# Activations stored as two halves, even and odd tokens, and read by the matmuls from both halves in turn

## The chip, the cores and the metric

The kernel runs on one core of one Trainium2 chip. The metric is the device time of one execution in microseconds (us), lower is better. The profile names the engines PE (TensorE matmuls), PEld (TensorE weight loads, which overlap PE), DVE (VectorE), ACT (ScalarE), POOL (GpSimd) and SP (SyncE, which issues most of the DMAs).

## The reference, cut to what matters

One decoder layer is computed for 288 tokens: a prompt of 256 tokens and 8 samples of 4 tokens. The width is 2048, the feed-forward width 5632.

```python
h = _rms(x, g_mix) * (1 + sc_m) + sh_m
proj = h @ w_in
b_gate, c_gate, hc, u, v, ga, gb = jnp.split(proj, idx, axis=-1)
# short convolution -> ya, spatial gating -> yb
merged = jax.nn.sigmoid(ga) * (ya @ w_pa) + jax.nn.sigmoid(gb) * (yb @ w_pb)
x = x + gt_m * (merged @ w_out)
h2 = _rms(x, g_ffn) * (1 + sc_f) + sh_f
gate, up = jnp.split(h2 @ w_ffn_in, 2, axis=-1)
x = x + gt_f * ((jax.nn.silu(gate) * up) @ w_ffn_out)
```

The shifts, scales and gates come from `silu(c) @ w_ada + b_ada`. Everything is in float32.

## The kernel before, in words

**Layout.** Activations are held transposed: features on the 128 partitions, tokens along the free axis. A tile of activations is therefore 128 x 288 (`T` = 288), and 128 x 298 (`TU`) where nine columns of modulation vectors and one of zeros ride along.

**The split matmul.** To keep float32 accuracy, each operand is split in two numbers of a shorter float type (`F32R`, fp32r in the profile): `hi`, a rounded copy, and `lo`, what is left. A product is three matmuls into one PSUM tile: weight hi by activation hi, weight hi by activation lo, weight lo by activation hi. The weight tile (128 x 128) is the stationary operand, the activation tile the moving one, read column by column.

- `Blk.run` (lines 464 to 478) is the main form. Lines 474, 475 and 476 are the three matmuls, inside a loop over output tiles and over the tiles of the contraction.
- `FirstBlk.run` (481 to 494) does the first block of w_in, with its matmul on line 492: 8 output tiles by three matmuls, all of 298 columns.
- `KBlk.run` (498 to 516) does the first four output tiles of the feed-forward input, in 4 blocks of 4 contraction tiles by 4 output tiles by three matmuls (lines 508 to 510), all of 298 columns.

**Where activation halves are made.** ACT copies to `hi`, DVE subtracts to `lo`. This is done in `split` (222), in `Modulate.high` and `Modulate.low` (271 and 275), in `modulate` (280) and in `early0` (583). `split` is called by `scaled` (249), `mix_conv` (675), `gate` in `spatial` (763), `sink_pb` (787) and `sink_fi` (829). Altogether 1 + 16 tiles of 298 columns are split and 16 + 16 + 8 + 8 + 16 + 44 = 108 tiles of 288. A split activation tile is read by every output tile of its matrix, so its two halves are made once and streamed into TensorE many times.

**Weights** are split likewise, in segments of up to 512 columns (`Blk.high`, 433, and `Blk.low`, 445). The change does not touch these.

**Other matmuls** are the modulation `Ada` (`Ada.run`, line 352, matmul on line 364), which reads unsplit float32 weights as the moving operand, and small sums, transposes and broadcasts. They read their operands as before.

**Order.** The order of the whole work is a hand-written list, `steps`. On DVE, ACT and SP a wrapper `Pinned` (line 103) keeps instructions in the written order until the list ends it; every instruction issued through it carries the line number 114 in the profile. On TensorE, `behind(S["pe"])` keeps blocks in order. Weights come by DMA from the SP queue, five buffers ahead (`RAW`).

Of the kernel before, what the change touches and what calls it, by code (L numbers as in the profile page):

```python
# [7 lines left out]
F32 = mybir.dt.float32  # L8
F32R = mybir.dt.float32r
ALU = mybir.AluOpType  # L10
AF = mybir.ActivationFunctionType

P = 128
D = 2048
T = 288
TP = 256
TU = T + 10
# [62 lines left out]
def _body(tc, nc, d, pc, pw, pslot, ptmp, pps):  # L80
    ids = [0]

    def nm(s):
        ids[0] += 1
        return f"{s}_{ids[0]}"
# [4 lines left out]
    def slot(dt=F32, shape=(P, T)):  # L90
        return pslot.tile(list(shape), dt, tag="s", name=nm("s"), padded_shape=[P, TU])

    def tmp(n=T):
        return ptmp.tile([P, n], F32, tag="t", name=nm("t"), padded_shape=[P, TU])

    def psmain():
        return pps.tile([P, 512], F32, tag="main", name=nm("pm"), bufs=4)

    def psmisc():
        return pps.tile([P, 512], F32, tag="misc", name=nm("px"), bufs=3)  # L100

    def behind(i):
        return tc.issue_after(i.ins) if i is not None else ExitStack()
# [17 lines left out]
    V, A, G, PE, SY = Pinned(nc.vector), Pinned(nc.scalar), nc.gpsimd, nc.tensor, Pinned(nc.sync)  # L121
# [94 lines left out]
    def sam(ap):  # L216
        return ap.rearrange("p (b s) -> p b s", s=NS)

    def bc4(ap):
        return ap.unsqueeze(2).to_broadcast([P, NB, NS])  # L220

    def split(a, n=T):
        hi = slot(F32R, (P, n))
        S["hi"] = A.copy(hi, a)
        lo = slot(F32R, (P, n))
        S["lo"] = V.tensor_tensor(lo, a, hi.bitcast(F32), ALU.subtract)
        return hi, lo

    def normed(kt, rb):
        t = slot()  # L230
# [3 lines left out]
    def in_order(i):  # L234
        if S["strict"]:
            S["pe"] = i
        return i
# [19 lines left out]
    class Modulate:  # L257
# [11 lines left out]
            S["aff"] = G.tensor_tensor(sam(h[:, TP:]), sam(h[:, TP:]), bc4(mod[:, sh, 1:]), ALU.add)  # L269

        def high(self):
            self.hi = slot(F32R)
            A.copy(self.hi, self.h)

        def low(self):
            lo = slot(F32R)
            V.tensor_tensor(lo, self.h, self.hi.bitcast(F32), ALU.subtract)
            self.out[self.k] = (self.hi, lo)

    def modulate(ks, get, gm, sh0, out):  # L280
        hs, his = {}, {}

        def affine(k, t):
            h = tmp()
            A.activation(
                h[:, :TP], t[:, :TP], AF.Identity, bias=mod[:, sh0 + k, 0:1], scale=gm[:, k, 0:1]
            )
            G.tensor_tensor(sam(h[:, TP:]), sam(t[:, TP:]), bc4(gm[:, k, 1:]), ALU.mult)  # L288
            S["aff"] = G.tensor_tensor(sam(h[:, TP:]), sam(h[:, TP:]), bc4(mod[:, sh0 + k, 1:]), ALU.add)  # L289
            hi = slot(F32R)  # L290
            A.copy(hi, h)
            hs[k], his[k] = h, hi

        def finish_(k):
            lo = slot(F32R)
            V.tensor_tensor(lo, hs[k], his[k].bitcast(F32), ALU.subtract)
            out[k] = (his[k], lo)

        ts = {}
        n = len(ks)  # L300
        for i in range(n + 2):
            if i < n:
                ts[i] = get(ks[i])
            if 1 <= i <= n:
                affine(ks[i - 1], ts.pop(i - 1))
            if i >= 2:
                finish_(ks[i - 2])
# [22 lines left out]
    class Ada(Step):  # L330
# [21 lines left out]
        def run(self):  # L352
            w, ks = self.nq * 128, self.ks
            if self.blk == 0:
                Ada.cur[self.name] = pps.tile([P, 512], F32, tag="ada", name=nm("ada"), bufs=1)
            acc = Ada.cur[self.name]
            for k, h in [(k, h) for k in range(self.nk // ks) for h in range(1 + self.apart)]:
                for j in range(4):
                    kt = self.blk * self.nk + k * ks + j % ks
                    o = (k * 4 + j) * w  # L360
                    c = slice(256 * h, 256 * h + 256) if self.apart else slice(0, w)
                    with behind(S.get("pe")):
                        self.last = in_order(
                            PE.matmul(  # L364
                                acc[32 * j : 32 * j + 32, c],
                                cs[:, kt, :],
                                self.raw[2 * j + h] if self.apart else self.raw[:, o : o + w],
                                start=(kt < ks),
                                stop=(kt >= 16 - ks),
                                tile_position=(0, 32 * j),  # L370
                                skip_group_check=True,
                            )
                        )
            if (self.blk + 1) * self.nk == 16 and not self.defer:
                self.tail()
# [31 lines left out]
    class Blk(Step):  # L407
# [56 lines left out]
        def run(self):  # L464
            cuts = self.cuts or [0, self.nk]
            acc = {}
            for a, b, j in [(a, b, j) for a, b in zip(cuts, cuts[1:]) for j in range(self.nm)]:
                ps = acc[j] if a else acc.setdefault(j, psmain())
                for k in range(a, b):
                    wh, wl = self.parts[j * self.nk + k]  # L470
                    ah, al = self.rhs(self.k0 + k)
                    first, last = k == 0, k == self.nk - 1
                    with behind(S.get("pe")):
                        PE.matmul(ps[:, : self.n], wh, ah, start=first, stop=False)  # L474
                    PE.matmul(ps[:, : self.n], wh, al, start=False, stop=False)  # L475
                    self.last = in_order(PE.matmul(ps[:, : self.n], wl, ah, start=False, stop=last))  # L476
                if b == self.nk:
                    self.sinks(j, ps)

    class FirstBlk(Blk):  # L480
        def run(self):
            ah, al = self.rhs(0)
            cuts = [0] + list(range(2, self.nm + 1))
            for a, b in zip(cuts, cuts[1:]):
                pss = [psmain() for _ in range(a, b)]
                for n in range(3):
                    for i, ps in enumerate(pss):
                        wh, wl = self.parts[a + i]
                        w, r = ((wh, ah), (wl, ah), (wh, al))[n]
                        with behind(S.get("pe")):  # L490
                            self.last = in_order(
                                PE.matmul(ps[:, : self.n], w, r, start=n == 0, stop=n == 2)
                            )
                for i, ps in enumerate(pss):
                    self.sinks(a + i, ps)

    class KBlk(Blk):
        def run(self):
            if self.idx == 0:
                S["kps"] = [psmain() if j else psmisc() for j in range(self.nm)]  # L500
            nb = 16 // self.nk
            for k in range(self.nk):
                ah, al = self.rhs(self.idx * self.nk + k)
                first, last = self.idx + k == 0, self.idx == nb - 1 and k == self.nk - 1
                for j in range(self.nm):
                    ps = S["kps"][j]
                    wh, wl = self.parts[k * self.nm + j]
                    PE.matmul(ps[:, :TU], wh, ah, start=first, stop=False)
                    PE.matmul(ps[:, :TU], wh, al, start=False, stop=False)
                    self.last = PE.matmul(ps[:, :TU], wl, ah, start=False, stop=last)  # L510
                for f in self.then.get(k, ()):
                    f()
            if self.idx == nb - 1:
                for j, ps in enumerate(S.pop("kps")):
                    self.sink(j, ps)
# [20 lines left out]
    S = {"strict": True}  # L536
# [46 lines left out]
    def early0():  # L583
        a = S["x0"] = tmp(TU)
        G.memset(a[:, T + NC :], 0.0)
        gain1(0, 1)
        V.tensor_scalar(a[:, :TP], x[:, 0, :TP], gm1[:, 0, 0:1], None, ALU.mult)
        V.tensor_tensor(sam(a[:, TP:T]), sam(x[:, 0, TP:]), bc4(gm1[:, 0, 1:]), ALU.mult)
        G.tensor_copy(a[:, T : T + NC], mod[:, 0, :])
        G.tensor_tensor(  # L590
            a[:, T + 1 : T + NC], a[:, T + 1 : T + NC], a[:, T : T + 1].to_broadcast([P, NB]), ALU.subtract
        )
        wA[0].high()
        hi = slot(F32R, (P, TU))
        A.copy(hi, a)
        wA[0].low()
        lo = slot(F32R, (P, TU))
        V.tensor_tensor(lo, a, hi.bitcast(F32), ALU.subtract)
        xe[0] = (hi, lo)
        wA[0].high()  # L600
        wA[0].low()

# [15 lines left out]
    xe, sq = {}, {}  # L618
# [387 lines left out]
    n = len(steps)  # L1006
# [163 lines left out]
```

## Time and profile before

| what | value |
|---|---|
| median of 3 runs | 1632.2 us (1631.9 to 1632.58) |
| profiled execution: span, the one time that its page gives | 1630.9 us |
| PE busy | 1618.2 us, 99% of the span |
| PEld busy | 1554.6 us, 95% |
| DVE busy | 995.3 us, 61% |
| ACT busy | 740.7 us, 45% |
| POOL busy | 121.2 us, 7% |
| read from HBM | 352.56 MB, 218 GB/s over the span |

The span is the stretch covered by the profiled execution's instructions. The median of the timed runs is 1.3 us longer. Matmuls are pipelined: the duration that the profile gives for one is the time from its start until its last result is written, and the next one starts well before that. So the cost of a matmul in a dense stream is read from the distance between starts, not from its duration. For groups, the columns are: line, engine, operation, out<-in, shapes and count; then busy time in us and mean ns of one; then idle time of the engine just before the group, and what ended it.

### The profile page before, as it was taken

Reading aid. Unit: us, or ns where it says so; the run is one execution under the profiler, and the core shown is the slowest. Engines: PE = TensorE matmul, PEld = TensorE weight load, DVE = VectorE, ACT = ScalarE, POOL = GpSimd, SP = SyncE. Lnnn points to the kernel's source line nnn. Section 1 sums busy time; section 2 is a strip of 40 time slices with the busy share of each in tenths; the row PEclk is TensorE's granted clock in tenths of the full one; section 3 lists DMA queues with packets and bytes.
Section 4 is the critical chain, followed back from the end, with each engine's and each line's share of the span. In section 5 each row is a group of like instructions: output and inputs, shape, how many; then the busy total and the mean of one; then the engine's idle time right before and its main releaser. Section 6 shows DMA issues by size and latency. Waiting matters only on the chain.

```text
span 1630.9 us, 31703 instructions
## 1 busy us (share of the span) xinstructions
PE 1618.2 (99%) x12584; PEld 1554.6 (95%) x12584; DVE 995.3 (61%) x2003; ACT 740.7 (45%) x1373; POOL 121.2 (7%) x251
## 2 busy tenths in 40 slices
PE   9999999999999999999999999999999999999997
PEld 7898899998999998999989899999999999999997
DVE  5776577877655566657845455555555555555565
ACT  5443354643444444446734344444444444344453
POOL 2267010000100000012200000000000000000000
PEclk9999999999999999999999999999999999999999
DMA  9877765766877777764588545443464434545342
GB/s 359 337 263 295 301 260 179 260 240 261 306 286 275 255 258 273 242 233 168 196 280 294 203 169 204 167 162 135 163 211 158 170 135 161 208 159 178 124 169 76
DMA packets 74468, 357.70 MB, mean 219 GB/s; under 512 B 8416, under 2 KB 28288, under 8 KB 44112
## 3 DMA queue, kind: packets, MB, share of 16 engines
q1 hardware_dynamic: 73968, 354.95, 60.6%
q8 instruction: 98, 1.61, 0.4%
q0 software_dynamic: 352, 0.73, 0.1%
q14 instruction: 50, 0.41, 0.1%
HBM read 352.56 MB, written 3.09 MB: 218 GB/s over the span
## 4 chain that ended last, share of the span: by engine, by line
issue 51%; ACT 0%; DVE 0%; POOL 0%; POOLq 0%; PE 0%; DVEq 0%
DVE x L114 0%; ACT hi L114 0%; ACT t L114 0%; ACT s L114 0%; POOL t L288 0%; POOL t L289 0%; PE px L211 0%; POOLq L1156 0%; DVE lo L114 0%; DVE s L114 0%; DVEq L1156 0%; DVEq L114 0%; POOLq L288 0%
## 5 line engine op out<-in xcount | busy, mean ns | idle before, releaser
L474 PE MATMUL pm<-s,hi 128*128 128x288 f32 (+1 forms) x3704 | 1094.4, 295 | 0.3 <-ACT s L114 0.2
L476 PE MATMUL pm<-s,lo 128*128 128x288 f32 (+1 forms) x3704 | 1090.3, 294 | 0.0
L475 PE MATMUL pm<-s,hi 128*128 128x288 f32 (+1 forms) x3704 | 1089.6, 294 | 0.0
L114 DVE TENSOR_TENSOR lo<-raw,hi 128x512 fp32r<-128x512 f32 (+1 forms) x966 | 662.2, 687 | 480.2 <-ACT hi L114 465.2
L114 ACT CAST hi<-raw 128x512 fp32r<-128x512 f32 (+1 forms) x966 | 587.0, 608 | 772.7 <-PE pm L475 735.7
L474 PEld LDWEIGHTS pm<-s,hi 128*128 128x128 f32 x3704 | 696.2, 188 | 11.8 <-issue 9.0
L475 PEld LDWEIGHTS pm<-s,hi 128*128 128x128 f32 x3704 | 696.5, 188 | 0.0
L476 PEld LDWEIGHTS pm<-s,lo 128*128 128x128 f32 x3704 | 696.0, 188 | 0.3 <-DVE lo L114 0.3
L364 PE MATMUL ada<-raw,cs 128*32 128x512 f32 (+3 forms) x768 | 75.6, 525 | 1.2 <-DMA raw<-in_aA 0.7
L114 DVE TENSOR_TENSOR s<-pm,s 128x288 f32<-128x288 f32 x128 | 58.1, 455 | 30.0 <-PE pm L476 29.5
L205 POOL TENSOR_TENSOR r<-r,mhalf 128x3 f32<-128x3 f32 x3 | 3.0, 996 | 883.8 <-DVE r L114 883.8
L114 ACT CAST s<-t 128x288 fp32r<-128x288 f32 (+1 forms) x109 | 46.9, 432 | 23.6 <-DVE t L114 19.5
L364 PEld LDWEIGHTS ada<-raw,cs 128*32 128x32 f32 x768 | 21.9, 110 | 36.8 <-issue 30.0
L114 DVE TENSOR_TENSOR s<-t,s 128x288 fp32r<-128x288 f32 (+1 forms) x109 | 50.0, 461 | 8.3 <-ACT s L114 8.3
L114 DVE SCALAR_TENSOR_TENSOR t<-t,pm 128x288 f32<-128x288 f32 x84 | 37.8, 451 | 15.9 <-PE pm L476 15.9
L114 DVE SCALAR_TENSOR_TENSOR x<-pm,mod,x 128x256 f32<-128x256 f32 x80 | 38.0, 475 | 0.0
L613 POOL TENSOR_TENSOR s<-s,rb 128x288 f32<-128x288 f32 x40 | 37.2, 932 | 0.0
L114 DVE TENSOR_TENSOR t<-pm,mod 128x32 f32<-128x32 f32 x80 | 15.3, 192 | 21.0 <-PE pm L476 21.0
L252 POOL TENSOR_TENSOR t<-x,gm 128x32 f32<-128x32 f32 x16 | 7.8, 490 | 268.9 <-DVE acc L114 255.7
L114 DVE SCALAR_TENSOR_TENSOR s<-pm,s 128x288 f32<-128x288 f32 x48 | 24.4, 511 | 0.5
L288 POOL TENSOR_TENSOR t<-s,gm 128x32 f32<-128x32 f32 x28 | 12.2, 437 | 154.1 <-DVE s L114 77.2
L114 ACT ACTIVATE t<-x 128x288 f32<-128x288 f32 x30 | 13.4, 445 | 20.1 <-DVE x L114 20.1
(126 smaller groups left out, 547.6 us busy)
## 6 DMA issues: line engine op xcount, KB each, us to landing
raw<-in_fi SPq DMA_DIRECT2D x84, 1024.0 KB, 4.9
raw<-in_a SPq DMA_DIRECT2D x48, 1024.0 KB, 4.9
raw<-in_f SPq DMA_DIRECT2D x64, 704.0 KB, 4.0
raw<-in_wD SPq DMA_DIRECT2D x36, 1024.0 KB, 8.5
raw<-in_wC SPq DMA_DIRECT2D x20, 896.0 KB, 6.7
raw<-in_aE SPq DMA_DIRECT2D x16, 1024.0 KB, 7.3
s<-in_a SPq DMA_DIRECT2D x128, 128.0 KB, 5.3
raw<-in_wo SPq DMA_DIRECT2D x16, 1024.0 KB, 5.7
```

What stands on the lines that cost most here:

```text
L114: i = f(*args, **kw)
L205: G.tensor_tensor(r, r, mhalf, ALU.pow)
L252: G.tensor_tensor(sam(a[:, TP:T]), sam(x[:, k, TP:]), bc4(gm[:, k, 1:]), ALU.mult)
L288: G.tensor_tensor(sam(h[:, TP:]), sam(t[:, TP:]), bc4(gm[:, k, 1:]), ALU.mult)
L364: PE.matmul(acc[32 * j : 32 * j + 32, c], cs[:, kt, :], self.raw[2 * j + h] if self.apart else self.raw[:, o : o + w], start=(kt < ks), st ...
L474: PE.matmul(ps[:, : self.n], wh, ah, start=first, stop=False)
L475: PE.matmul(ps[:, : self.n], wh, al, start=False, stop=False)
L476: self.last = in_order(PE.matmul(ps[:, : self.n], wl, ah, start=False, stop=last))
L613: G.tensor_tensor(a[:, :T], a[:, :T], S[rb], ALU.mult)
```

## The change: what it does

Two views are defined. `pair` looks at a tile of n columns as n/2 pairs of neighbours; walked in its order it is the natural order of the columns. `turn` looks at a tile as two halves of n/2 columns and walks them in turn: column 0 of the first half, column 0 of the second, column 1 of the first, and so on.

Every `hi` and `lo` tile of activations is now written through `turn` while the source is read through `pair`. So the first half of the tile holds the even tokens, the second half the odd ones. Every split matmul reads its moving operand through `turn`, so its columns come in natural order, and the PSUM tile and all that follows it stay as they were. In the moving operand, neighbouring columns lie n/2 elements apart: 144 x 4 = 576 bytes, or 149 x 4 = 596 bytes for 298 columns. `lo` is subtracted with source, `hi` and result walked in this way.

No instruction is added, removed or moved in the written order; only access patterns change. The weights, the `Ada` matmuls and the small matmuls keep theirs.

```diff
+    def turn(t, n=T):
+        return t[:, :n].rearrange("p (a b) -> p b a", a=2)
+
+    def pair(t, n=T):
+        return t[:, :n].rearrange("p (b a) -> p b a", a=2)
+
+    def upper(a, n=T):
+        hi = slot(F32R, (P, n))
+        A.copy(turn(hi, n), pair(a, n))
+        return hi
+
+    def lower(a, hi, n=T):
+        lo = slot(F32R, (P, n))
+        V.tensor_tensor(turn(lo, n), pair(a, n), turn(hi.bitcast(F32), n), ALU.subtract)
+        return lo
+
     def split(a, n=T):
-        hi = slot(F32R, (P, n))
-        S["hi"] = A.copy(hi, a)
-        lo = slot(F32R, (P, n))
-        S["lo"] = V.tensor_tensor(lo, a, hi.bitcast(F32), ALU.subtract)
-        return hi, lo
+        hi = upper(a, n)
+        return hi, lower(a, hi, n)
...
         def high(self):
-            self.hi = slot(F32R)
-            A.copy(self.hi, self.h)
+            self.hi = upper(self.h)
 
         def low(self):
-            lo = slot(F32R)
-            V.tensor_tensor(lo, self.h, self.hi.bitcast(F32), ALU.subtract)
-            self.out[self.k] = (self.hi, lo)
+            self.out[self.k] = (self.hi, lower(self.h, self.hi))
...
-                    ah, al = self.rhs(self.k0 + k)
+                    ah, al = (turn(t, self.n) for t in self.rhs(self.k0 + k))
...
-            ah, al = self.rhs(0)
+            ah, al = (turn(t, self.n) for t in self.rhs(0))
...
-                ah, al = self.rhs(self.idx * self.nk + k)
+                ah, al = (turn(t, TU) for t in self.rhs(self.idx * self.nk + k))
```

`modulate` and `early0` are changed in the same way, to call `upper` and `lower`.

More of the change, by code (lines that the diff above doesn't have):

```diff
@@ L289, in affine @@
             S["aff"] = G.tensor_tensor(sam(h[:, TP:]), sam(h[:, TP:]), bc4(mod[:, sh0 + k, 1:]), ALU.add)
-            hi = slot(F32R)
-            A.copy(hi, h)
-            hs[k], his[k] = h, hi
+            hs[k], his[k] = h, upper(h)
         def finish_(k):
-            lo = slot(F32R)
-            V.tensor_tensor(lo, hs[k], his[k].bitcast(F32), ALU.subtract)
-            out[k] = (his[k], lo)
+            out[k] = (his[k], lower(hs[k], his[k]))
         ts = {}
@@ L593, in early0 @@
         wA[0].high()
-        hi = slot(F32R, (P, TU))
-        A.copy(hi, a)
+        hi = upper(a, TU)
         wA[0].low()
-        lo = slot(F32R, (P, TU))
-        V.tensor_tensor(lo, a, hi.bitcast(F32), ALU.subtract)
-        xe[0] = (hi, lo)
+        xe[0] = (hi, lower(a, hi, TU))
         wA[0].high()
```

## The prediction

> **What bounds the kernel now.** I read the page first: the span, the busy shares and the row of the granted clock.
>
> ```profile
> span 1630.9 us, 31703 instructions
> PE 1618.2 (99%) x12584; PEld 1554.6 (95%) x12584; DVE 995.3 (61%) x2003; ACT 740.7 (45%) x1373; POOL 121.2 (7%) x251
> PEclk9999999999999999999999999999999999999999
> ```
>
> PE has 12.7 us of idle time in 1630.9, and its clock is full throughout. A busy PE is not yet PE at its peak, so next I read the table of busy time by stretch, in which the columns after each stretch are PE, PEld, DVE, ACT and POOL with their counts, then clock, DMA share and GB/s.
>
> ```profile
> 100.00:300.00 200.00, 199.53 (x1529) 186.23 (x1532) 136.07 (x246) 85.95 (x157) 59.46 (x98) 1.00 0.66 241
> 1200.00:1500.00 300.00, 300.00 (x2276) 300.00 (x2275) 163.37 (x303) 131.17 (x229) 0.00 (x0) 1.00 0.49 169
> 1600.00:1631.00 31.00, 21.08 (x161) 20.50 (x159) 16.04 (x38) 9.51 (x19) 0.86 (x1) 0.88 0.20 77
> ```
>
> In the middle PE never stops, while DVE works 68% of the time at its busiest (136.07 of 200) and DMA has room. Most of PE's idle time lies in the last stretch (9.9 us). What does one matmul cost there? The timeline of PE alone, from 1000 us on, gives the distance between starts; between the first and the last of these rows lie 31 distances.
>
> ```profile
> 999.80 0.29 PE L476 MATMUL pm<-s,lo 128*128 128x288 f32 x1
> 999.93 0.30 PE L474 MATMUL pm<-s,hi 128*128 128x288 f32 x1
> ...
> 1003.88 0.29 PE L474 MATMUL pm<-s,hi 128*128 128x288 f32 x1
> ```
>
> 4.08 us over 31 is **131.6 ns from start to start**, for 288 columns. It is the same for hi and for lo, and nothing ends a wait: the groups of matmuls, kept apart by shape, show 0.3 us of idle time in all.
>
> ```profile
> L474 PE MATMUL pm<-s,hi 128*128 128x288 f32 x3664 | 1082.1, 295 | 0.3 <-ACT s L114 0.2
> L364 PE MATMUL ada<-raw,cs 128*32 128x512 f32 x512 | 59.2, 595 | 0.5 <-DMA raw<-in_aE 0.5
> L364 PE MATMUL ada<-raw,cs 128*32 128x256 f32 x128 | 7.7, 382 | 0.0
> ```
>
> So the kernel is bound by the rate at which TensorE streams moving columns, and the change touches just this operand. Whatever one column costs more is paid in full; there is no cover. Lines 474, 475 and 476 have 3664 matmuls each of 288 columns, 10992 in all, and 40 each of 298 columns (the "+1 forms" of the page's 3704), which makes 120. By the code, line 492 adds 24 and lines 508 to 510 add 192 of 298 columns: 336. Together **11328 matmuls** are changed.
>
> **The price of a column, from rows.** The two rows of line 364 are unsplit float32 matmuls: 256 columns more take 595 - 382 = 213 ns more, 0.832 ns per column, and a fixed part of 595 - 512 x 0.832 = 169 ns remains. Taking the same fixed part off the 295 ns of line 474 leaves 126 ns for 288 columns, **0.4375 ns per column**. The split matmuls thus stream almost twice as fast (1.9 times), and of the 131.6 ns between starts 5.6 are not columns. This is an estimate across two shapes of matmul (32 and 128 columns of weights), but it gives the scale.
>
> **The change part by part.**
>
> *The moving reads.* Now neighbouring columns are neighbours in memory; afterwards each column lies 576 bytes (596 for 298) from the one before, and the second next lies beside the first. No row shows a moving operand read with a step, so its cost is bounded from both sides. Below, it is nothing, or a gain of the 5.6 ns, if these were caused by the order of the reads. The nearest row is that of the float32 matmul, at 0.832 ns per column: a slower rate at which this engine is seen to stream. I take it: two neighbouring columns that arrive together now would then arrive one after the other, and each fetch bring one useful column. The far end is four times today's column, 1.75 ns, if a fetch brings four columns now and three of them are thrown away.
>
> At 0.832 ns the added time per column is 0.832 - 0.4375 = 0.3945 ns: 113.6 ns for 288 columns, 117.6 ns for 298. 10992 x 113.6 ns = 1248.7 us, 336 x 117.6 ns = 39.5 us. **Sum: 1288 us.** Starts would be 131.6 + 113.6 = 245.2 ns apart.
>
> [...]
>
> *The writes of hi and lo.* ACT and DVE now write with a step, and DVE reads hi with one.
>
> ```profile
> L114 ACT CAST s<-t 128x288 fp32r<-128x288 f32 x92 | 39.6, 432 | 22.7 <-DVE t L114 19.5 <-POOL t L289 2.7
> L114 DVE TENSOR_TENSOR s<-t,s 128x288 fp32r<-128x288 f32 x92 | 41.8, 457 | 2.9 <-ACT s L114 2.9
> PEld pm L474 <- ACT s L114: 1.4, 3, 0.6
> ```
>
> 92 such pairs, with 17 of 298 columns and 16 merged ones 125 in all by the code. Their price is bounded by nothing below and, by the row of the float32 matmul again as the nearest slower stream (1.9 times), by about as much again: 0.43 us on ACT and 0.46 on DVE each, 54 and 57 us in sum. What hides it is the busy PE: ACT is idle for 890 us of the span and DVE for 636, and a pair is made long before its matmul. Only where PE waits for a half does it show: 0.9 us for the first tile (`early0`), and 3 waits of line 474 on ACT, with 0.43 us each, 1.3 us. So it is worth 0 to 2.2 us; I take 0, since with a slower PE these two engines get further ahead. If their cover went in some stage, the whole 57 us would be the price.
>
> *Order, DMA, weights.* No instruction, wait or DMA is added or moved, so no queue is passed. The DMA queue follows the buffers that PE frees; it only has more time. PE's idle 12.7 us at both ends stay.
>
> **The sum.** On the profiled execution: 1630.9 + 1288.2 = 2919.1 us. Its page gives no time besides the span; the median of the runs is 1.3 us above it, and with these 1.3 the forecast is **2920 us**.
>
> **The rivals.**
>
> - *Four times the column.* A fetch brings four neighbouring columns today, and afterwards one. For it: nothing in the trace says how many columns a fetch brings, and 4 x 0.4375 is as good a whole multiple as 2 x. Against it: no matmul is seen to stream so slowly, and the row of 512 float32 matmuls has 512 x 595 ns = 305 us of durations in 59.2 us of busy time, so about five overlap, each on its own moving tile: the memory feeds several places at once. The column costs 1.75 ns: +378 ns for 288, +391 for 298; 10992 x 378 = 4155 us and 336 x 391 = 131 us. 1632.2 + 4286 = 5919 us. If the whole 131.6 ns were multiplied by four: 394.8 ns and 408.5 ns more, 4340 + 137 us, 6109 us.
> - *No difference on PE.* The read path keeps two places open: the second next column is the neighbour of this one, so each half is read in order, and nothing is fetched twice. For it: the overlapping float32 matmuls above, fed from several places at once. [...] Then only the writes are left: 1632 to 1634.4 us.
> - *A part of the step.* The price of the hop is partly hidden in the flow, or only one of the streams pays it: anything from 1636 to 2857 us; by half the step, 56.8 ns per matmul, some 2276 us.
> - *Faster.* The 5.6 ns per matmul that are not columns are a collision of the moving read with the weight load beside it (PEld is busy 300 of 300 us in the stretch from 1200), and reading from two places in turn avoids it. All of it gone gives 11328 x 5.6 ns = 63 us, 1569 us. It decides from 0.29 ns per matmul on (3.3 us over 11328). Against it: the weights are read as before and in the same number, so a collision with them would have no reason to go.
> - *The change does nothing.* The views could cancel out, if a compiler folded them into one. The tile is written in one order and read in another, so both steps have to exist; I give this nothing of its own.
>
> **How the numbers follow.** Chances: one column per two of today's 0.39, four times 0.27, a part 0.11, no difference 0.16, faster 0.07. The likeliest gives 2920 us; its own range reaches from 2857 (two-cycle columns with nothing else between: 239.6 - 131.6 = 108 ns, and 111.7 for 298) to 3124 us (all of the 131.6 ns doubled, 136.2 for 298). Leaving out both the faster case and that of no difference would leave out 0.23, so the range starts at 1629, where no difference ends, and reaches to 6109, the upper end of the fourfold case. It holds 0.93; the bounds of the one unknown price make it so wide. A measurement of this kernel can tell 0.2% (3.3 us) from no change. Slower by over that: 0.39 + 0.27 + 0.11 = 0.77; within: 0.16; faster: 0.07.
>
> **What would show it.** Right: the groups of lines 474 to 476 have 169 + 240 = 409 ns where they had 295, starts lie 245 ns apart in the timeline, and line 364 stays at 595 ns. For the fourfold case the duration would be 673 ns, the distance 510; for no difference 295 and 131.6, with only the casts of ACT and the subtractions of DVE longer. The casts of 288 columns between 432 and 860 ns would settle the second price. Wrong would be the forecast if lo and hi differed in distance, if the granted clock fell, or if PE began to wait for ACT or DVE: then the cost would lie in the writes and not in the reads.

## The result and the profile after

| | before | with the change |
|---|---|---|
| median | 1632.16 us (1631.9 to 1632.58, 4 runs) | **1533.73 us** (1533.47 to 1536.78, 4 runs) |
| ratio | | **0.94** (95% interval 0.9387 to 0.9413) |

The kernel became 98.4 us faster; 2920 us had been forecast. The profiled execution is the slowest of the four, 1536.78 us with a span of 1535.0.

The page of the changed kernel, first the engines, then the three groups that the change touches in the most places. In it the three matmuls of `Blk.run` stand at lines 480, 481 and 482 (474, 475 and 476 before).

```profile
span 1535.0 us, 31703 instructions
PE 1515.9 (99%) x12584; PEld 1448.1 (94%) x12584; DVE 1010.8 (66%) x2003; ACT 763.1 (50%) x1373; POOL 122.9 (8%) x251
...
L480 PE MATMUL pm<-s,hi 128*128 128x288 f32 (+1 forms) x3704 | 1063.5, 287 | 1.0 <-ACT s L114 0.8
L481 PE MATMUL pm<-s,hi 128*128 128x288 f32 (+1 forms) x3704 | 1059.7, 286 | 1.1 <-DVE s L114 1.1
L482 PE MATMUL pm<-s,lo 128*128 128x288 f32 (+1 forms) x3704 | 1060.1, 286 | 0.5 <-DVE lo L114 0.3
```

PE is still busy all the time with as many instructions, but one matmul is shorter: 286 ns from start to last result, where it was 295. The timeline of PE at the same place as before gives the distance; between the first and the last row lie 34.

```profile
999.81 0.29 PE L481 MATMUL pm<-s,hi 128*128 128x288 f32 x1
999.93 0.29 PE L482 MATMUL pm<-s,lo 128*128 128x288 f32 x1
...
1003.98 0.29 PE L482 MATMUL pm<-s,lo 128*128 128x288 f32 x1
```

4.17 us over 34 is **122.6 ns, 9.0 ns less** than 131.6. The table by stretch says nearly the same: from 1200 to 1500 us there are 2452 matmuls where there were 2276, at 122.3 ns each instead of 131.8. Its row for 700 to 800 us is shown below from the kernel before and then from the changed one, with the row for 1200 to 1500 us last.

```profile
700.00:800.00 100.00, 100.00 (x752) 100.00 (x752) 74.70 (x165) 66.27 (x142) 26.11 (x81) 1.00 0.51 179
700.00:800.00 100.00, 96.88 (x767) 94.81 (x766) 76.84 (x154) 69.22 (x136) 20.48 (x57) 1.00 0.61 208
1200.00:1500.00 300.00, 300.00 (x2452) 300.00 (x2451) 185.90 (x348) 152.80 (x264) 0.00 (x0) 1.00 0.52 176
```

The first two rows show the other side: PE, which had been busy for all of that stretch before, now idles for 3.1 us. (The faster kernel is further on in its work there; the kernel `e_read` below, with the same reads and plain writes, idles for 0.8 us.) The writes of hi and lo did become dearer, by two thirds and by half.

```profile
L114 ACT CAST s<-t 128x288 fp32r<-128x288 f32 x92 | 64.2, 706 | 27.0 <-DVE t L114 23.7 <-POOL t L299 3.0
L114 DVE TENSOR_TENSOR s<-t,s 128x288 fp32r<-128x288 f32 x92 | 61.6, 675 | 8.2 <-ACT s L114 7.6
```

A second thing in the distances answers a question that the prediction had not asked. Before, they were not noise: in the feed-forward input each of the 48 matmuls of an output tile had its own distance, from 126 to 140 ns, and kept it within 1 ns from one output tile to the next (so for 99% of the distances between 1000 and 1100 us). So it hung on which tiles were read. Between 950 and 1060 us of the changed kernel every distance is 122 or 123.

### The profile page after: what moved, and what is told of

It reads as the page before. It is cut to its first block, busy times and chain, and to the rows that moved or that the text cites. A ratio compares the mean times of both kernels' runs of the same rounds, so it can differ in the third digit from the quotient of the medians.

```text
span 1535.0 us, 31703 instructions
## 1 busy us (share of the span) xinstructions
PE 1515.9 (99%) x12584; PEld 1448.1 (94%) x12584; DVE 1010.8 (66%) x2003; ACT 763.1 (50%) x1373; POOL 122.9 (8%) x251
## 4 chain that ended last, share of the span: by engine, by line
issue 50%; DVE 1%; ACT 0%; POOL 0%; POOLq 0%; PE 0%; DVEq 0%
DVE x L114 0%; DVE s L114 0%; ACT s L114 0%; DVE lo L114 0%; POOL t L298 0%; POOL t L299 0%; ACT t L114 0%; PE px L211 0%; POOLq L1159 0%; DVEq L1159 0%; ACT hi L114 0%; DVEq L114 0%; POOLq L298 0%
## 5 line engine op out<-in xcount | busy, mean ns | idle before, releaser
L480 PE MATMUL pm<-s,hi 128*128 128x288 f32 (+1 forms) x3704 | 1063.5, 287 | 1.0 <-ACT s L114 0.8
L481 PE MATMUL pm<-s,hi 128*128 128x288 f32 (+1 forms) x3704 | 1059.7, 286 | 1.1 <-DVE s L114 1.1
L482 PE MATMUL pm<-s,lo 128*128 128x288 f32 (+1 forms) x3704 | 1060.1, 286 | 0.5 <-DVE lo L114 0.3
L114 ACT CAST s<-t 128x288 fp32r<-128x288 f32 (+1 forms) x109 | 76.3, 707 | 27.9 <-DVE t L114 23.7
L114 DVE TENSOR_TENSOR s<-t,s 128x288 fp32r<-128x288 f32 (+1 forms) x109 | 73.9, 682 | 15.9 <-ACT s L114 15.3
L617 POOL TENSOR_TENSOR s<-s 128x32 f32<-128x32 f32 x48 | 23.3, 488 | 0.0
## 6 DMA issues: line engine op xcount, KB each, us to landing
s<-in_a SPq DMA_DIRECT2D x128, 128.0 KB, 5.6
```

The costliest lines, as they stand in the source:

```text
L114: i = f(*args, **kw)
L617: G.tensor_tensor(sam(a[:, TP:T]), sam(a[:, TP:T]), bc4(a[:, T + 1 : T + NC]), ALU.add)
```

## The experiments

**First: the reads or the writes, and a bench of streams.** There are four kernels. Two make one half of the change each; the code is shown as cuts, against the changed kernel.

```diff
 # e_read: written plainly, read in turn
-        A.copy(turn(hi, n), pair(a, n))
+        A.copy(hi, a[:, :n])
-        V.tensor_tensor(turn(lo, n), pair(a, n), turn(hi.bitcast(F32), n), ALU.subtract)
+        V.tensor_tensor(lo, a[:, :n], hi.bitcast(F32), ALU.subtract)
 # e_write: written as in the change, read plainly (so in all three forms of Blk)
-                    ah, al = (turn(t, self.n) for t in self.rhs(self.k0 + k))
+                    ah, al = (t[:, : self.n] for t in self.rhs(self.k0 + k))
```

> Half of the change: hi and lo are written plainly, and the split matmuls read them in turn. So the tokens come out in another order (0, 144, 1, 145, ...) and what is done by token afterwards is done to the wrong ones. If the whole gain is in the moving reads, starts lie 122.6 ns apart, ACT's casts are back at 432 ns and DVE's subtractions at 457, and the kernel takes 1528 to 1533.5 us, at or a little below the changed one. If the layout of the tile in memory matters to the gain as well as the order of reads, it stays above 1533.

Measured: 1528.6 us (1528.14 to 1529.08), ratio to before 0.9359 (0.9345 to 0.9373). The distance is 122.5 ns, and the casts are back at their old length:

```profile
L114 DVE TENSOR_TENSOR s<-t,s 128x288 fp32r<-128x288 f32 x92 | 41.7, 456 | 4.0 <-ACT s L114 4.0
L114 ACT CAST s<-t 128x288 fp32r<-128x288 f32 x92 | 39.5, 431 | 27.1 <-DVE t L114 23.0 <-POOL t L299 3.9
```

> The other half: hi and lo are written in two halves as in the change, and the split matmuls read them plainly, column after column. The tokens come out with the even ones first. If the gain is in the moving reads alone, starts lie 131.6 ns apart again and the kernel takes 1632 to 1637 us, as before or a little slower for the longer casts (706 and 675 ns). Any part of the 98 us that stays would belong to the writes.

Measured: 1636.53 us (1635.62 to 1637.69), ratio 1.0023 (1.0013 to 1.0032); the median distance of the 288-column matmuls is 132 ns, as before. So the whole gain, 104 us, lies in the order of the moving reads, and the longer casts cost 4 to 5 us of it.

The third kernel puts rows of 64 matmuls behind the last store of the changed kernel, one row to a line, for example

```python
for i in R: PE.matmul(Q[i // 16][:, :288], W[:, 0:128], M[:, 0:288], **S1[i])
for i in R: PE.matmul(Q[i // 16][:, :288], W[:, 0:128],
                      M[:, 0:288].rearrange("p (a b) -> p b a", a=2), **S1[i])
```

with one weight tile `W` and one moving tile `M`. (`**S1[i]` only says where a sum in PSUM starts and stops.)

> The changed kernel, and behind its last store 42 rows of 64 matmuls each of fp32r data that nothing else reads, one row to a line of the source; ACT, DVE and DMA are idle there. Distances from start to start count. In the kernel a plain read of 288 columns took 131.6 ns and the read in turn 122.6 ns. Theory L (reach of the read path): a plain stream must open the next 16 bytes every four columns and is a little late each time; read in turn each place serves eight columns. It expects 131 to 132 ns for every plain row whatever the weights and offsets, with the weights narrowed to 32 columns too; 122.6 for halves in turn at any distance and for runs of two; about 131 again for runs of four and eight; slower than 131 for step 2 and step 4. Theory W (collision with the weight load that runs beside): a plain row depends on where the weights lie against the moving tile, so the rows with offsets spread between 126 and 140 ns, and with 32 columns of weights the plain row falls to about 122.6. Theory O (collision with the other engines and DMA): every plain row is at 122.6, since nobody else reads or writes. For quarters, sixths and eighths L gives 122.6 as long as the path keeps so many places open, and twice as much or more beyond that.

Groups of PE by line. A row's distance is its busy time less one duration, over 63 (line 887: (8.0 - 0.286) / 63 = 122.4 ns). Line 887 reads in turn; 895 plainly; 900 plainly with weights of 32 columns; 903 in runs of four, 902 in runs of two; 907 eighths; 908 step 2, first all even and then all odd columns; 922 and 923 are 512 columns, plain and in turn. Plain stands for line 895 and not for the first row of the bench, line 886, because that one began at a granted clock of 0.5; all the rows used ran at 1.00.

```profile
L908 PE MATMUL pm<-mov,wgt 128*128 128x288 f32 x64 | 16.7, 437 | 0.0
L907 PE MATMUL pm<-mov,wgt 128*128 128x288 f32 x64 | 15.9, 424 | 0.0
L922 PE MATMUL pm<-mov,wgt 128*128 128x512 f32 x64 | 14.7, 389 | 0.0
L923 PE MATMUL pm<-mov,wgt 128*128 128x512 f32 x64 | 14.0, 379 | 0.0
L902 PE MATMUL pm<-mov,wgt 128*128 128x288 f32 x64 | 12.1, 356 | 0.0
...
L903 PE MATMUL pm<-mov,wgt 128*128 128x288 f32 x64 | 8.9, 302 | 0.0
...
L895 PE MATMUL pm<-mov,wgt 128*128 128x288 f32 x64 | 8.6, 294 | 0.0
...
L900 PE MATMUL pm<-mov,wgt 128*32 128x288 f32 x64 | 8.6, 294 | 0.0
L887 PE MATMUL pm<-mov,wgt 128*128 128x288 f32 x64 | 8.0, 286 | 0.0
```

From the starts, plain 131.7 ns, narrow weights 131.1, in turn 122.5 at each of seven distances of the halves, runs of four 136.6, runs of two 186.7, quarters 153.3, sixths 166.7, eighths 246.7, step 2 257.8. This rules out O (no other engine is at work, and plain is still 131.7) and the strong form of W (a quarter of the weight columns saves 0.6 ns). L got the runs of two wrong, for which it wanted 122.6, and has no price like 153.3 for the quarters; and its excess should have grown from 9.2 ns at 288 columns to 16 at 512, where it is 11.

The fourth kernel writes and reads its tiles in runs of two columns.

> The change with runs of two: tiles of 288 columns hold columns 0, 1, 4, 5, ... in one half and 2, 3, 6, 7, ... in the other, and are read two columns from one half, two from the other; tiles of 298 stay as in the change. Theory L: each place still serves its four columns within eight, so 122.6 ns and 1530 to 1534 us; and if the writes were dear because single columns went to different places, the casts fall from 706 to about 432 ns and the subtractions from 675 to about 457. Theory W has no reason for another distance than the change's either, unless the collisions need single columns to be avoided: then 126 to 132 ns and 1565 to 1632 us.

Measured: 2219.52 us, ratio 1.3591 (1.3569 to 1.3614). The casts came down to 455 and the subtractions to 464 ns, as expected, but each matmul stands 185.6 ns from the next. L falls: in its picture runs of two serve each place as well as single columns do. W had expected no more than 132.

```profile
L484 PE MATMUL pm<-s,hi 128*128 128x288 f32 x3664 | 1328.9, 363 | 0.0
...
L114 DVE TENSOR_TENSOR s<-t,s 128x288 fp32r<-128x288 f32 x92 | 42.5, 464 | 2.7 <-ACT s L114 2.7
L114 ACT CAST s<-t 128x288 fp32r<-128x288 f32 x92 | 41.6, 455 | 16.5 <-DVE t L114 12.2 <-POOL t L303 1.5
```

**Second: what a feed sees.** Suppose that fp32r columns come to TensorE over two paths, called feeds here, one for the even columns and one for the odd, and that a feed has to open each new stretch of 16 bytes that it enters (the 16 is supposed here; the third bench measures it). Order the rows by what the even columns alone see, and they fall into line. In turn they run through one half without a gap; plain they take every second element; with step 2 every fourth; in runs of two they hop between the halves. That is theory H. It was put against two rivals in a second bench.

> The changed kernel and, behind its last store, rows of 64 matmuls on data that nothing else reads, with the other engines idle. The first set of rows (plain 131.7 ns, in turn 122.5 at any distance, 136.6 in runs of four, 186.7 in runs of two, 258 for step 2, 247 for eighths, and only 11 ns between plain and turn for 512 columns) felled the collisions with weight load or engines, and the old theory L: the excess does not grow with the columns. Theory H (two feeds, hits per line): even and odd columns come over two feeds; each opens a new 16 bytes every 1.7 ns at most, and one that takes only two elements from each runs just at that limit and cannot catch up what it loses at the start of an instruction. In turn it takes four. H expects: turn with step 2 inside the halves 131 to 137 ns, step 4 some 258; two plain blocks in a two-level pattern 131 to 137; every column twice, and pairs two, three or four apart, 122.5; plain and turn by turns 127; 298 to 448 columns 9 to 11 ns more plain. In bf16 plain takes four already: 122.5 plain and turn, 131 to 137 step 2, 258 steps 4 and 8. Theory S (shape): an inner count of two starts cheaper, wherever it points: 122.5 for turn with step 2 and 4, bf16 plain at 131. Theory C (the feeds collide in the same 16 bytes): turn with step 2 122.5, every column twice and pairs two apart 131 or more, pairs four apart 122.5.

| row | distance, ns | H | S | C |
|---|---|---|---|---|
| in turn, step 2 in the halves | 131.8 | yes | no | no |
| in turn, step 4 | 255.5 | yes | no | |
| two plain blocks | 133.4 | yes | | |
| every column twice | 122.5 | yes | yes | no |
| pairs two, three, four apart | 123.3, 122.5, 122.5 | yes | yes | no |
| plain and turn by turns | 126.8 | yes | | |
| 298: plain, in turn | 139.8, 126.7 | nearly | | |
| 384: plain, in turn | 173.3, 162.5 | yes | | |
| 448: plain, in turn | 202.6, 189.2 | nearly | | |
| bf16 plain, step 2, step 4 | 122.5, 126.7, 256 | nearly | no | |
| bf16 in turn, step 8 | **273.3, 506.7** | **no, no** | no | |

Line 916 is bf16 in turn, at a granted clock of 1.00.

```profile
L916 PE MATMUL pm<-m,w 128*128 128x288 bf16 x64 | 17.7, 435 | 0.0
```

S and C fall. H holds for fp32r and fails for bf16: reading in turn is more than twice as slow there, and one element per 16 bytes costs 507 ns and not 258. The second is what one feed instead of two would give, twice the openings; the first fits one feed as well, which must hop between the halves, but its size is not explained.

**Third: the rate of one feed.** So theory R: fp32r comes over two feeds by even and odd columns, bf16 over one, and each feed can open a new 16 bytes every 1.75 ns, an estimate from the 506.7 ns that 288 columns of bf16 with step 8 took (1.76 each).

> Rows of 64 matmuls of 288 columns behind the last store, as before, now with the step varied. What the rows before showed: fp32r in turn with step 2 131.8 ns, step 4 255.5; bf16 plain 122.5, step 2 126.7, step 4 256, step 8 506.7, and in turn 273. So theory H was wrong on bf16: there all columns come over one feed, and only fp32r has two, by even and odd columns. Theory R (rate): each feed opens a new 16 bytes every 1.75 ns, and a matmul takes the longer of its columns (122.5 ns) and its number of new lines per feed times 1.75 ns. Then what counts is bytes per step: fp32r in turn with step 3 opens 0.75 lines per column of a feed, 144 x 0.75 x 1.75 = 189 ns; with step 4 and 5 one, 252 to 258. fp32r with plain steps 2, 3 and 4: one line per column of a feed, 252 to 260. bf16 with step 3: 0.375 lines per column, 189 ns; 4: 252 to 256; 5: 315; 6: 378; 7: 441; 8 and 10: 504 to 507. Rival theory D (doubling): the rate falls only by whole halves, so step 3 costs as much as 4 (256) in bf16 and in fp32r in turn, and 5, 6 and 7 as much as 8 (507).

Groups of the third bench; 906 to 914 are bf16 with steps 1, 2, 3, 4, 5, 6, 7, 8 and 10, line 900 is fp32r in turn with step 3 and 901 with step 4.

```profile
L914 PE MATMUL pm<-m,w 128*128 128x288 bf16 x64 | 33.0, 692 | 0.0
L913 PE MATMUL pm<-m,w 128*128 128x288 bf16 x64 | 32.6, 685 | 0.0
...
L911 PE MATMUL pm<-m,w 128*128 128x288 bf16 x64 | 24.6, 560 | 0.0
...
L909 PE MATMUL pm<-m,w 128*128 128x288 bf16 x64 | 16.5, 435 | 0.0
L908 PE MATMUL pm<-m,w 128*128 128x288 bf16 x64 | 12.5, 357 | 0.0
L907 PE MATMUL pm<-m,w 128*128 128x288 bf16 x64 | 8.3, 288 | 0.0
L906 PE MATMUL pm<-m,w 128*128 128x288 bf16 x64 | 8.0, 286 | 0.0
```

```profile
L901 PE MATMUL pm<-mov,wgt 128*128 128x288 f32 x64 | 16.5, 436 | 0.0
L900 PE MATMUL pm<-mov,wgt 128*128 128x288 f32 x64 | 12.5, 363 | 0.0
```

The distances, in the order of the steps: 122.5, 126.7, 193.3, 256, 320, 381.3, 445, 506.7 and 513.3 ns; fp32r in turn with step 3 193.3, steps 4 and 5 255.6 and 260; fp32r with plain steps 2, 3 and 4 255.6, 256.6 and 261.3. From step 2 on, each extra 2 bytes of step cost 61 to 67 ns up to 16 bytes, and the next 4 bytes only 6.6: this is the 16 that the theories had supposed. D, the rival, wanted 256 at step 3 and 507 at step 5. R fits, with an estimate of 1.76 ns for each opening (506.7 / 288).

The granted clock tells more about this price. In this bench it was 1.00 up to step 4 and 0.50 from step 7 on, and it changed within the rows between. That left no mark: in step 5 the distance was 319.9 ns at 1.00 and 320.0 at 0.50, in step 6 381.5 and 381.3. The columns do follow the clock. The first plain fp32r row of each bench began at 0.50, and its matmuls stood 240 ns apart there, twice the 120 that the columns alone take at 1.00 (288 of 0.4165 ns, by the rows in turn of 288 and 512 columns), without any excess; at 1.00 they stood 131.7 ns apart. So in these rows what R calls an opening costs a time and does not follow the clock, and the plain read shows it at 1.00 (131.7 against 122.5 in turn) and not at 0.50 (240).

R prices the plain fp32r read (a line is 16 bytes): each feed opens all 72 lines, 72 x 1.76 = 126.7 ns, **4.2 ns more than its columns take**. In turn each feed opens 36, 63 ns, far under the 122.5. What is left of the excess is 131.7 - 126.7 = 5 ns. The next bench searches for it.

> Rows of 64 matmuls of 288 columns behind the last store, to find the other half of a plain read's excess. Theory R (a new 16 bytes per feed each 1.76 ns) gives a plain fp32r read 72 x 1.76 = 126.7 ns, as seen for bf16 with step 2 and once for fp32r in turn with step 2; the plain rows lie at 131 to 136 ns, and in turn with step 2 was 131.8 another time. Both have two feeds that open a line every second column. Theory F (the two feeds hinder each other by where they point): the rows in turn with step 2 change between 126.7 and 140 ns with the distance of the two halves alone, and stay so with weights of 32 columns. Theory W (the openings of a feed at its limit are hindered by the weight load): the distance of the halves makes no difference, but the place of the weights does, and with 32 columns of weights the rows come nearer to 126.7. Theory A (start inside a 16-byte line: one line more, 73 instead of 72): only starts that are no multiple of four elements are dearer, by 1.8 ns. Reads in turn with step 1 stay at 122.5 from each start, since they have time to spare.

| in turn with step 2, halves so many elements apart | distance, ns |
|---|---|
| 576, 640, 704, 1024 (multiples of 64) | 131.7, 131.6, 131.6, 131.6 |
| 578, 580, 582 | 133.3, 133.3, 136.7 |
| 584, 608 | **126.7, 126.7** |
| 588, 592, 600 | 128.9, 128.3, 128.9 |

Lines 902 and 906 are the rows at 576 and at 584.

```profile
L902 PE MATMUL pm<-mov,wgt 128*128 128x288 f32 x64 | 8.6, 294 | 0.0
L906 PE MATMUL pm<-mov,wgt 128*128 128x288 f32 x64 | 8.3, 288 | 0.0
```

At 576 with the start of both halves moved by 2, 4 and 8 elements the distance is 133.3, 131.8 and 133.4. With weights of 32 columns the rows at 576, 578, 580 and 584 are 131.1, 133.6, 130.0 and 128.0; with the weights moved, 132.0 to 133.3. Reads in turn from 2, 4 and 8 stay at 122.5.

| plain, from element | 0 | 2 | 4 | 6 | 8 |
|---|---|---|---|---|---|
| distance, ns | 131.7 | 134.4 | 131.6 | 135.6 | 133.4 |
| with weights of 32 columns | 131.1 | 133.3 | 133.2 | 130.0 | 130.0 |

F is what the first table says: from 576 to 584, both of them whole numbers of 16 bytes, the distance of the two feeds' places alone moves the row from 131.7 to 126.7, just R's price. In F's picture a plain read is the case where both feeds want the same 16 bytes; it costs what halves a multiple of 64 apart cost, 131.7 and 131.6 ns. But F is not all. Weights of 32 columns instead of 128 shift a row by up to 5.6 ns, in both directions (plain from 6: 135.6 to 130.0; from 4: 131.6 to 133.2), so W may have a part of it. A has perhaps one too: plain starts at 2 and 6 are dearer by 2.7 and 3.9 ns, where A wanted 1.8, and so is bf16 with step 2, which in R has one feed and no neighbour to hinder it, from element 4: 130.0 ns against 126.7 from 0 and 8. Against A, the plain start at 8 is dearer as well.

**Fourth: does each instruction pay for itself?** Only the lo tiles of the activations are kept in two halves and read in turn; hi stays plain. The cut shows the main form of `Blk`. The other two are changed likewise, and lo is written half after half, as in the fifth experiment.

```diff
-                    ah, al = (turn(t, self.n) for t in self.rhs(self.k0 + k))
+                    ah, al = self.rhs(self.k0 + k)
+                    al = turn(al, self.n)
```

> Only the lo tiles of the activations are kept in two halves and read in turn (one of the three matmuls of a split product, weight hi by activation lo); hi stays plain. The output is that of the change. If the excess of a plain read is paid by each instruction by itself, a third of the gain comes: 10992 x 9.2 ns and 336 x 13 ns make 105.5 us, a third is 35 us, 1595 to 1600 us. If the start of an instruction pays for the one before it or after it, or the three share what they lose, it is another part: 1632 for none, down to 1562 us where one matmul in turn spares two.

Measured: 1602.61 us (1602.54 to 1603.68), ratio 0.9817 (0.98 to 0.9833): 30 us, a little less than a third and 3 us above the range expected for it. Over all distances between 100 and 150 ns, the middle matmul went from 131.9 to 122.3 ns, but its two plain neighbours went from 132.1 and 132.0 to 132.7 and 133.0. 9.6 ns gained and 1.6 lost, times 3704, is 30 us. Mostly each pays for itself.

```profile
L484 PE MATMUL pm<-s,hi 128*128 128x288 f32 x3664 | 1085.2, 296 | 0.3 <-ACT s L114 0.2
L486 PE MATMUL pm<-s,lo 128*128 128x288 f32 x3664 | 1082.8, 296 | 0.1
L485 PE MATMUL pm<-s,hi 128*128 128x288 f32 x3664 | 1045.3, 285 | 0.0
```

**Fifth: the same tiles, written in another order.** The longer casts write single elements to two places by turns. The same copy can walk the halves one after the other and read every second element instead.

```diff
     def pair(t, n=T):
-        return t[:, :n].rearrange("p (b a) -> p b a", a=2)
+        return t[:, :n].rearrange("p (b a) -> p a b", a=2)
+
+    def halves(t, n=T):
+        return t[:, :n].rearrange("p (a b) -> p a b", a=2)
...
-        A.copy(turn(hi, n), pair(a, n))
+        A.copy(halves(hi, n), pair(a, n))
...
-        V.tensor_tensor(turn(lo, n), pair(a, n), turn(hi.bitcast(F32), n), ALU.subtract)
+        V.tensor_tensor(halves(lo, n), pair(a, n), halves(hi.bitcast(F32), n), ALU.subtract)
```

> The same tiles and the same reads as in the change, but ACT and DVE walk them in another order: first all even tokens, then all odd ones. So hi and lo are written column after column, and the source is read at every second element. The output is that of the change. If the longer casts (706 against 432 ns) and subtractions (675 against 457) come from writing single elements to two places, they fall to 432 to 500 and 457 to 520 ns and the kernel takes 1528 to 1531 us, faster than the changed one's 1533.7. If reading every second element costs as much, nothing is won: 1532 to 1536 us.

Measured: **1528.95 us** (1528.31 to 1529.74, 5 runs), ratio to before 0.9366 (0.9354 to 0.9379), faster than both kernels. The casts take 467 ns and the subtractions 457, and in the stretch from 700 us PE idles for 0.9 us instead of 3.1.

```profile
L114 ACT CAST s<-t 128x288 fp32r<-128x288 f32 x92 | 42.8, 467 | 26.7 <-DVE t L114 23.0 <-POOL t L302 3.5
L114 DVE TENSOR_TENSOR s<-t,s 128x288 fp32r<-128x288 f32 x92 | 41.9, 457 | 4.2 <-ACT s L114 4.2
```

## Why the prediction was wrong

**What bounds the kernel: right.** The kernel was bound by the stream of moving columns and what a column costs was paid, or gained, in full: 10992 x 9.0 ns is 99 us, and 336 matmuls of 298 columns at 13 ns less make 4; together 103, against the 104 us of `e_read`.

**The step that failed is "two neighbouring columns that arrive together now would then arrive one after the other, and each fetch bring one useful column".** It took the stream for one path whose fetches are shared by neighbouring columns. The rows behave as two paths in fp32r (one element per 16 bytes 255.6 ns, and 506.7 in bf16), and in this picture the change gives each of them a stretch without gaps: from each 16 bytes a feed now takes four elements where it took two. So the change would have halved the number of openings per feed where I had let it grow. At the estimated 1.76 ns an opening this accounts for 4.2 of the 9.0 ns gained; the other 5 go with where the two reads point (126.7 to 136.7 ns in the fourth bench, 122.5 for in turn from every start), and their mechanism stays open. The price of 0.832 ns per column is real, but it belongs to other patterns: step 2 measured 257.8 ns, 0.895 per column, and the forecast distance of 245 is that of eighths (246.7).

**The price of a column was mis-sized too.** The fixed part of 169 ns was nearly right, but all that it left of 295 was taken for columns, 126 ns, and only 5.6 of the distance for the rest. In turn, 288 and 512 columns take 286 and 379 ns, 0.415 ns per column: 119.6 ns are columns, and 166 a fixed part. (The 0.832 ns of the float32 rows, "two-cycle columns" in the prediction's range, is twice this; no run counts cycles.) So 12 of the 131.6 ns were not columns, and the change took 9.0 of them: 7% of each matmul stood open where I saw 4%.

**The rivals.** "Faster", at 0.07, had the right place and sign, an excess in each matmul that the new order avoids, and gave 63 us, but not the cause: it blamed a collision with the weight load, and with narrow weights the plain row stays at 131.1 ns. Other starts shift by up to 5.6 ns with them, so the weights may have a part, but not the main one. What I held against it, that nothing about the weights changed, was true and beside the point. "No difference" rested on two places kept open; what the rows fit is two feeds. "Four times the column" is about what bf16 shows where, in R, its one feed opens a line per column: 506.7 against 122.5 ns.

**The order of reads.** How many columns share a fetch was a guess; no row of the kernel before showed a moving read with a step. The rows show a kink at 16 bytes of step (506.7 ns at 16 bytes, 513.3 at 20), but to share 16 bytes is not enough: bf16 with step 4 takes two elements from each and 256 ns for 122.5, and with step 2, four elements, it still takes 126.7. In R's picture what decides is whether the columns streamed while a feed stays on a line last as long as an opening: four columns for a plain fp32r read and for bf16 with step 2, 1.67 ns and so just under 1.76, eight for fp32r in turn, 3.3 ns.

**The writes.** Their price was bounded well (0 to 0.43 and 0.46 us more; 0.27 and 0.22 measured) but their cover was trusted too much: 0 to 2.2 us forecast, 4 to 5 measured (`e_write` 1636.53 against 1632.54, the change 1533.73 against `e_read` 1528.6). The wait is not at the first tiles alone, where I had put it. Against `e_read`, with the same reads, PE is busy 95.3 instead of 97.7 us in the first 100 us, where line 370 alone waits 2.0 us for its DMA and not 0.3, which leaves some 0.7 us to the casts, and 96.9 instead of 99.2 us between 700 and 800 us, where lines 514 and 516 wait 0.7 us for hi from ACT and 1.0 us for lo from DVE.

**What stays open.** Two feeds are a picture that fits the rows and whose step prices held when put ahead of the run; no run shows the paths themselves. Open is also why the rows in turn with step 2 change with the distance of the halves as they do, alike (131.6 and 131.7 ns) at all four multiples of 64 elements; what the place of the weights and the start within a line add; why one feed that hops between two places costs what it does (runs of two 186.7, quarters 153.3 and bf16 in turn 273 ns, between R's prices with and without a kept line); and which tiles of the kernel gave which of the distances between 126 and 140 ns, since no run shows the addresses of its tiles.

## What to carry to other kernels

Distances from start to start that repeated within 1 ns, tile by tile, and lay 7% above the 122.6 ns of the read in turn were no noise here but came with where and in which order things were read, and a row of 64 matmuls per pattern, on data that nothing else reads, showed it in one run. For fp32r moving operands, let the even and the odd columns come from two gapless stretches (122.5 ns for 131.7 at 288 columns); do not carry this to bf16 or to runs of two, where it took 2.2 and 1.4 times as long as a plain read (273.3 for 122.5, 186.7 for 131.7). Note the granted clock of each row: at 0.50 a plain read took 240 ns and showed no excess at all. And when a tile is to be written in another order, turn the loop of the copy so that its writes run on and the reads take the step: here 467 and 457 ns for 706 and 675.

## What the runs showed of the hardware that was not expected

- The fp32r rows behave like two feeds, even and odd columns, the bf16 rows like one: in turn 122.5 against 273.3 ns, and one element per 16 bytes 255.6 against 506.7 ns for 288 columns.
- Between steps of 4 and 16 bytes in bf16 the distance grew by about 63 ns for every 2 bytes (126.7 to 506.7), and from 16 to 20 bytes by 6.6; an estimate from the 506.7 ns is 1.76 ns for each new 16 bytes. Step 5 took the same at a granted clock of 1.00 and of 0.50 (319.9 and 320.0 ns), where a plain fp32r read took 131.7 and 240 ns.
- In turn with step 2, the distance of the halves moved a row: 126.7 ns at 584 and 608 elements, 131.6 and 131.7 at multiples of 64, 136.7 at 582. Plain starts at 2 and 6 elements took 134.4 and 135.6 ns for the 131.7 at 0, and weights of 32 columns shifted a row by up to 5.6 ns, up or down (135.6 to 130.0, 131.6 to 133.2).
- ACT and DVE writing single elements to two places by turns take 706 and 675 ns for 288 elements, where plain writing took 432 and 457. In runs of two it is 455 and 464, and 467 and 457 where the writes are gapless and the source is read at every second element.
